# Two more parts of a modulation vector summed by VectorE instead of TensorE, in a hybrid attention, HGRN2 and MLP step

## The chip, the core and the metric

The kernel runs on one core of a Trainium2 chip. The metric is the time of one execution in microseconds (us), measured on the device; the number quoted is the median of several runs. Everything below that speaks of durations, waits or the clock comes from one profiled execution of the kernel before the change, read through views of its trace.

The engines are named as the views name them: PE is TensorE's matmuls, PEld its loads of the stationary operand, DVE is VectorE, ACT is ScalarE, POOL is GpSimd, and SP is the engine whose queue issues most transfers.

## The reference

The step takes 128 prompt tokens and 256 latent tokens (384 in all, 2048 features) through two layers. What matters here is the modulation of layer 0: six vectors of 2048 values for each of two conditioning vectors.

```python
m = jax.nn.silu(cvec) @ w_ada_l + b_ada_l              # w_ada_l: 2048 x 12288
sh1, sc1, g1, sh2, sc2, g2 = jnp.split(m, 6, axis=-1)
h = modulate(x, norm_mix, sh1, sc1)                    # rmsnorm(x) * gain * (1 + sc1) + sh1
x = x + g1 * mixer_ab(h, w_in, w_out, ...)             # attention (8 heads) beside HGRN2 (8 heads)
h = modulate(x, norm_mlp, sh2, sc2)
x = x + g2 * mlp(h, w1, w2)                            # 2048 -> 8192 -> 2048, squared ReLU
```

So SH1 and SC1 are needed first, G1 at the output projection, SH2 and SC2 at the norm ahead of layer 0's MLP, and G2 at the MLP's first outputs. Layer 1 is a pooling mixer and a second MLP. All arithmetic is in float32.

## The kernel before

The weights stream through the core once, as items of 1 MB, in a list that the host code writes out (`self.items`). Each item of a weight matrix (`w_unit`) is 1024 x 256; each of its two halves is split into a high and a low part, the high part by ScalarE (`split_hi`, L159) and the low part by VectorE (`split_lo`, L166), and TensorE then makes three products for each block of 128 features (`mm3`, L247 to L250): high by high, low by high, high by low, 384 tokens wide. Splits run four halves ahead of the products. The raw items have a ring of three buffers, the split ones five halves.

The order on every engine is the order in which the host code issues instructions; nothing reorders them. Work beside the main products sits in queues of generators (`queues`); `tick` adds a nominal time for each block of products, and a generator's next piece is issued when its yield has passed. `HY` is the yield between two steps of an HGRN2 head. A step (L859 to L868 and L841) is a chain: three products on TensorE (tile `pl`), two multiplications and one small product of totals on VectorE (`arr`, `tot`), a masked copy out of PSUM on VectorE (`att`), and a copy on ScalarE (`kh`) that the next step's products need. Attention is a longer chain for each head: scores (`s`) on TensorE, maxima on VectorE, exponentials on ScalarE, `prob` scaled on VectorE, transposes (`t`) on TensorE, copies out of PSUM by ScalarE and VectorE (`probt`), products with the values (`pov`).

The modulation's weights are items of another kind (`a_unit`) in the same list. There are two ways to sum them.

- `ada_pe`: an item is 512 rows x 512 columns; the two condition vectors are stationary and TensorE sums, in four column groups of 32 (L413, tile `psa`). One item is eight matmul records; four items make a block, 16 a part.
- `ada_dve`: an item is 256 rows x 1024 columns; VectorE multiplies and adds it into an accumulator `adaacc` of 128 x 2 x 1024, four instructions for an item (L473 for the first two of a block, L475 for the others); after eight items TensorE sums over the partitions (L489, eight records) and the result is folded (`ada_fold`).

In both, an item of this kind is handled in `split_hi`, so its instructions are issued at the start of a half of a weight item, four halves ahead of their neighbours in the list:

```python
if it["kind"] == "a":
    it["half"][half] = raw.rearrange("p (k c) -> p k c", k=k // 2)
    if "pool" not in it:
        it["proc"](half, it["half"][half])
    return
```

Before the change SH1, SC1, G1, SH2, SC2 and G2 of layer 0 all take `ada_pe`: the first two in the start-up, the other four (64 items) spread evenly between the items of the projections (`hgrn_jobs`, `att_jobs`, `gate_jobs`: 42 more items after the start-up) and of the output projection (`out_jobs`: 16 items). Layer 1's six parts take `ada_dve`, beside layer 0's MLP (`mlp_jobs`), with the accumulator in the MLP's pool.

PSUM: four accumulators `acc`, two buffers `ps_bg` shared by all background work, one `ps_s`, one `ps_a`.

Of the kernel before, what the change touches and what calls it, by code (L numbers as in the profile page):

```python
# [42 lines left out]
HY = (3.1, 3.1, 2.5, 3.1)  # L43
# [7 lines left out]
def _const_arrays():  # L51
# [28 lines left out]
    # the sums and the order of modulation rows: [block, v, group, chunk] and [block, v, chunk] -> [v, all chunks]  # L80
# [33 lines left out]
class Model:  # L114
    def __init__(self, ctx, tc, a):
        self.ctx, self.tc, self.nc, self.a = ctx, tc, tc.nc, a
        self.items = []
        self.pend = []
        self.sqs = []
        self.queues = {"e": [], "h": [], "q": [], "f": []}  # L120
        self.now = 0.0

    # ---------------------------------------------------------------- streams of weights
# [17 lines left out]
    def split_hi(self, j):  # L141
        """the high part on ScalarE; the low part's subtraction follows with split_lo."""
# [29 lines left out]
    def task(self, queue, gen, delay=0.0):  # L172
        """work beside the main products: each yield gives the time that its other engines need."""
        self.queues[queue].append([gen, self.now + delay])

    def later_on(self, fn):
        """the part of an evac that waits for ScalarE: VectorE comes to it a little later."""
# [108 lines left out]
    def quarter(self, w, c0, q, proc, pre=None):  # L286
        """half a unit: a quarter of the features, 256 columns."""
# [10 lines left out]
    def start_units(self, w, specs, pre=None):  # L298
        """the first products of a phase, a quarter of the features at a time, as these become known."""
# [50 lines left out]
    def job_tok(self, w, c0, evac):  # L350
        """out[tokens, 256 features] of w[:, c0:c0+256]."""
# [30 lines left out]
    # ---------------------------------------------------------------- adaLN  # L382
# [3 lines left out]
    def ada_done(self, layer, which, chunk0, n, ps):  # L386
        """ps [128, n, 2]: sums for n chunks of 128 features; adds the bias, folds gains in."""
# [12 lines left out]
    def ada_pe(self, layer, which, block, each=None, then=None):  # L400
        """512 columns of one part; the condition vectors are stationary, in four column groups."""
# [4 lines left out]
        def make(u):  # L406
            def proc(half, raw):
# [11 lines left out]
                if u == 3 and half == 1:  # L419
# [8 lines left out]
                    else:  # L428
                        if block == 0:
                            self.folded = self.small.tile([P, P], F32, name="folded", tag="folded", bufs=2)  # L430
                        for v in range(2):
                            at = block * 32 + v * 16
                            nc.gpsimd.dma_start(self.folded[at:at + 16], rows[v::32].rearrange("j (n c) -> j n c", n=4))
                        if block == 3:
                            self.task("f", self.ada_fold(layer, which, 0, P, self.folded), 6.5)
# [23 lines left out]
    def ada_dve(self, layer, which, block):  # L459
        """1024 columns of one part; multiply-adds on VectorE, the sum over partitions on TensorE."""  # L460
# [4 lines left out]
        def make(u):  # L465
            def proc(half, raw):
                kc = u * 2 + half
                if kc == 0:
                    st["acc"] = self.mlpp.tile([P, 2, 1024], F32, name="adaacc", tag="adaacc")
# [11 lines left out]
        def finish():  # L481
            if block == 0:
                self.folded = self.small.tile([P, P], F32, name="folded", tag="folded", bufs=2)
            folded = self.folded
            psr = self.ps_a.tile([P, 512], F32, name="psa", tag="a")
# [17 lines left out]
    # ---------------------------------------------------------------- set-up  # L503
# [922 lines left out]
```

## Time and profile before

| | |
|---|---|
| runs | 3127.81, 3128.39, 3129.56 us |
| median | 3128.39 us |
| span of the profiled execution | 3127.1 us |
| TensorE, share of the span | 98% |
| VectorE, share of the span | 58% |
| ScalarE, share of the span | 37% |
| mean granted TensorE clock | 0.996 |

The profiled span is 1.3 us under the median. Shares of busy time are averages over stages, so they tell only where to look: the projections lie at about 160 to 690 us of the span, the output projection with attention at 690 to 873 us, layer 0's MLP at 895 to 1895 us. The granted clock is a share of full speed: 1 is 2.4 GHz, 0.5 is 1.2 GHz.

### The profile page before, as it was taken

The page shows a single profiled execution, that of the slowest core. Times are in us where ns is not written, and L with a number is a line of the kernel's source. Part 1 is how long each engine was busy: PE and PEld are TensorE (multiplying, and loading weights), DVE is VectorE, ACT ScalarE, POOL GpSimd, SP SyncE. Part 2 cuts the span into 40 slices and gives each one's busy share as a digit, 9 for nine tenths or more (in the row PEclk, how much of TensorE's full clock was granted, in tenths as well). Part 3 has the DMA queues.
Part 4 walks back from the last instruction along what each step waited for, and adds up shares of the span by engine and source line. Part 5 has one row for each costly group of instructions (what it writes and reads, how often), then busy time and mean ns, then how long its engine had stood idle before and what let it go on. Part 6 is the DMA issues. An engine that isn't in the chain of part 4 may idle for free.

```text
span 3127.1 us, 43503 instructions
## 1 busy us (share of the span) xinstructions
PE 3064.3 (98%) x18106; PEld 2915.5 (93%) x18106; DVE 1821.8 (58%) x2557; ACT 1147.1 (37%) x1721; POOL 54.1 (2%) x93
## 2 busy tenths in 40 slices
PE   6999999999999999999999999899999999999997
PEld 3798889878899999999999999799999999999997
DVE  2455555545468888888978874754334343443434
ACT  3343333333362323333232333562333323233233
POOL 1100000000000000000000000000000000000000
PEclk9999999999999999999999999999999999999999
DMA  9866655565647767767767764243434434344342
GB/s 343 293 211 204 194 193 186 190 218 176 196 149 236 233 224 231 234 222 232 238 218 241 229 217 133 75 128 122 134 122 127 129 122 134 122 127 130 122 134 83
DMA packets 419460, 566.92 MB, mean 181 GB/s; under 512 B 10816, under 2 KB 338480, under 8 KB 418240
## 3 DMA queue, kind: packets, MB, share of 16 engines
q1 hardware_dynamic: 408672, 542.86, 53.6%
q0 software_dynamic: 5104, 13.65, 1.3%
q10 hardware_dynamic: 5488, 7.62, 0.8%
q8 instruction: 143, 2.34, 0.3%
q14 instruction: 53, 0.43, 0.0%
HBM read 556.13 MB, written 7.60 MB: 180 GB/s over the span
## 4 chain that ended last, share of the span: by engine, by line
PE 94%; ACT 2%; DVE 2%; DMA 1%; issue 0%; ACTq 0%; SPq 0%; DVEq 0%
PE acc L247 28%; PE acc L250 28%; PE acc L248 28%; PE psa L413 3%; PE pl L859 1%; PE acc L367 1%; PE acc L368 1%; PE acc L369 1%; ACT sp L159 1%; ACT hfull L667 0%; DVE sp L166 0%; PE acc L269 0%; PE psa L489 0%; DMA xtok<-in_x_sample 0%; PE pov L1092 0%
## 5 line engine op out<-in xcount | busy, mean ns | idle before, releaser
L159 ACT ACTIVATE sp<-raw 128x1024 fp32r<-128x1024 f32 x656 | 694.4, 1059 | 1473.9 <-PE acc L250 1204.9
L166 DVE TENSOR_TENSOR sp<-raw,sp 128x1024 fp32r<-128x1024 f32 x656 | 793.9, 1222 | 634.0 <-ACT sp L159 633.5
L247 PE MATMUL acc<-hh,sp 128*128 128x384 f32 x2720 | 923.4, 339 | 5.6 <-ACT sp L159 2.5
L248 PE MATMUL acc<-hh,sp 128*128 128x384 f32 x2720 | 910.6, 335 | 0.6 <-DVE sp L166 0.6
L250 PE MATMUL acc<-hl,sp 128*128 128x384 f32 x2720 | 691.9, 335 | 0.0
L247 PE MATMUL acc<-hid,sp 128*128 128x384 f32 x2032 | 685.7, 337 | 0.0
L248 PE MATMUL acc<-hid,sp 128*128 128x384 f32 x2032 | 683.8, 337 | 0.0
L247 PEld LDWEIGHTS acc<-hh,sp 128*128 128x128 f32 x2720 | 511.5, 188 | 51.8 <-issue 38.6
L250 PE MATMUL acc<-hid,sp 128*128 128x384 f32 x2032 | 518.6, 336 | 0.0
L248 PEld LDWEIGHTS acc<-hh,sp 128*128 128x128 f32 x2720 | 511.6, 188 | 1.0 <-DVE sp L166 1.0
L250 PEld LDWEIGHTS acc<-hl,sp 128*128 128x128 f32 x2720 | 491.8, 188 | 0.0
L475 DVE SCALAR_TENSOR_TENSOR adaacc<-raw,cpad,adaacc 128x1024 f32<-128x1024 f32 x360 | 438.4, 1277 | 0.0
L247 PEld LDWEIGHTS acc<-hid,sp 128*128 128x128 f32 x2032 | 381.4, 188 | 5.2 <-issue 5.0
L248 PEld LDWEIGHTS acc<-hid,sp 128*128 128x128 f32 x2032 | 381.4, 188 | 0.0
L250 PEld LDWEIGHTS acc<-hid,sp 128*128 128x128 f32 x2032 | 367.4, 188 | 0.0
L752 DVE SCALAR_TENSOR_TENSOR x<-acc,mods,x 128x128 f32<-128x128 f32 x576 | 200.4, 409 | 137.0 <-PE acc L250 135.1
L679 DVE TENSOR_TENSOR hid<-rsq,hid 128x384 fp32r<-128x384 f32 x128 | 65.7, 555 | 226.1 <-ACT hid L678 226.1
L413 PE MATMUL psa<-raw,cpad 128*32 128x512 f32 x768 | 112.6, 610 | 2.4 <-ACT adarow L423 1.4
L841 ACT ACTIVATE kh<-arr 128x384 f32<-128x384 f32 x56 | 31.2, 557 | 182.0 <-DVE arr L864 86.8
L864 DVE TENSOR_TENSOR arr<-arr,tot 128x384 f32<-128x384 f32 x96 | 49.2, 554 | 43.7 <-PE pl L859 42.4
L367 PE MATMUL acc<-sp,hh 128*128 128x256 f32 x240 | 73.2, 305 | 0.0
L1183 ACT ACTIVATE rsq<-relu 128x384 f32<-128x384 f32 x128 | 67.4, 526 | 4.1
(271 smaller groups left out, 2013.4 us busy)
## 6 DMA issues: line engine op xcount, KB each, us to landing
raw<-in_w_ada SPq DMA_DIRECT2D x192, 1024.0 KB, 5.1
raw<-in_w_mlp_out SPq DMA_DIRECT2D x128, 1024.0 KB, 5.4
raw<-in_w_mlp_in SPq DMA_DIRECT2D x120, 1024.0 KB, 5.6
raw<-in_w_in_ab SPq DMA_DIRECT2D x42, 1024.0 KB, 5.6
raw<-in_w_out_ab SPq DMA_DIRECT2D x16, 1024.0 KB, 5.6
raw<-in_w_in_ab POOLq DMA_DIRECT2D x17, 512.0 KB, 5.9
raw<-in_w_mlp_in SPq DMA_DIRECT2D x16, 512.0 KB, 3.7
raw<-in_w_pool SPq DMA_DIRECT2D x4, 1024.0 KB, 5.3
```

The source lines that it names most:

```text
L159: self.nc.scalar.activation(sp[:, 0], raw, AF.Copy)
L166: self.nc.vector.tensor_tensor(sp[:, 1], raw, sp[:, 0].bitcast(F32), op=ALU.subtract)
L247: mm(ps[:, :T], sp[:, 0, kc, c], hi, start=first, stop=False)
L248: mm(ps[:, :T], sp[:, 1, kc, c], hi, start=False, stop=False)
L250: mm(ps[:, :T], sp[:, 0, kc, c], lo, start=False, stop=last)
L367: nc.tensor.matmul(ps, hi, sp[:, 0, kc], start=(gk == 0), stop=False)
L413: nc.tensor.matmul(st["ps"][32 * j:32 * j + 32], self.cpad[:, kc], raw[:, k], start=(u == 0), stop=(u == 3))
L475: nc.vector.scalar_tensor_tensor(st["acc"][:, v], raw[:, 0], s, st["acc"][:, v], op0=ALU.mult, op1=ALU.add)
L679: nc.vector.tensor_tensor(lo, full, hi.bitcast(F32), op=ALU.subtract)
L752: nc.vector.scalar_tensor_tensor(self.x[:, kc, t0:t0 + n], ps[:, t0:t0 + n], g[:, kc, v:v + 1], self.x[:, kc, t0:t0 + n], op0=ALU.mult, op ...
L864: nc.vector.tensor_tensor(x, x, m, op=ALU.mult)
L1183: nc.scalar.activation(q[o], r[o], AF.Square)
```

## The change

SH2 and SC2 of layer 0 go from `ada_pe` to `ada_dve`: 32 items of 512 x 512 for TensorE become 32 items of 256 x 1024 for VectorE, in four blocks. 20 of them are spread over the 42 items of the projections, 12 over the output projection. The accumulator gets a pool of its own (`accp`), opened with the projections. G1 is spread over the projections alone; half of G2 goes to the output projection and half to the first eight items of the MLP, all by `ada_pe`. Layer 1's items end eight items before the end of the MLP instead of twelve. `HY` grows by 0.4. The sum over partitions uses a buffer of `ps_bg` instead of `ps_a`. The scratch for transfers issued by GpSimd is set to 8192 bytes. Line numbers grow by one or two.

```diff
-HY = (3.1, 3.1, 2.5, 3.1)
+HY = (3.5, 3.5, 2.9, 3.5)
...
     def ada_dve(self, layer, which, block):
...
                 if kc == 0:
-                    st["acc"] = self.mlpp.tile([P, 2, 1024], F32, name="adaacc", tag="adaacc")
+                    st["acc"] = self.accp.tile([P, 2, 1024], F32, name="adaacc", tag="adaacc")
...
         def finish():
             if block == 0:
-                self.folded = self.small.tile([P, P], F32, name="folded", tag="folded", bufs=2)
-            folded = self.folded
-            psr = self.ps_a.tile([P, 512], F32, name="psa", tag="a")
+                self.folded[layer, which] = self.small.tile([P, P], F32, name="folded", tag="folded", bufs=3)
+            folded = self.folded[layer, which]
+            psr = self.ps_bg.tile([P, 512], F32, name="psa", tag="bg")
...
     def open_mix(self):
...
+        self.accp = self.ctx.enter_context(self.tc.tile_pool(name="accp", bufs=1))
...
     def build(self):
...
-        for which in (G1, SH2, SC2, G2):
-            for b in range(4):
-                self.ada_pe(0, which, b)
...
+        def spread(body, *extras):
+            out, done = [], [0] * len(extras)
+            for n, it in enumerate(body):
+                for e, (u, lo, hi) in enumerate(extras):
+                    want = min(max(n - lo, 0) * len(u) // (hi - lo), len(u))
+                    out += u[done[e]:want]
+                    done[e] = want
+                out.append(it)
+            return out + [it for d, (u, _, _) in zip(done, extras) for it in u[d:]]
...
+        g2, norm2 = pe(G2), dve((0, SH2), (0, SC2))
+        w_in, w_out = n1 - n0, n2 - n0
+        self.items = mix[:n0] + spread(mix[n0:], (pe(G1), 0, w_in - 4), (g2[:8], w_in - 4, w_out),
+                                       (norm2[:20], 0, w_in), (norm2[20:], w_in, w_out - 2))
+        late = dve(*[(1, which) for which in range(6)])
+        self.items += spread(rest, (g2[8:], 0, 8), (late, 9, n3 - 8))
...
-    nc = _bacc.Bacc("TRN2", target_bir_lowering=False, num_devices=1)
+    nc = _bacc.Bacc("TRN2", target_bir_lowering=False, num_devices=1, dynamic_dma_scratch_size=8192)
```

The first place is VectorE's queue in the projections, in the first HGRN2 head of the second pair, where the third pair of weight columns (`hq`) is evacuated. Before:

```order
L864 TENSOR_TENSOR arr<-arr,tot 128x192x2 x2
L868 TENSOR_TENSOR tot<-tot 128x192
L846 COPY_PREDICATED att<-masks_134,pl 128x384
L166 TENSOR_TENSOR sp<-raw,sp 128x1024
L785 TENSOR_TENSOR hq<-acc,sig 128x384 x2
L864 TENSOR_TENSOR arr<-arr,tot 128x96x4 x2
L868 TENSOR_TENSOR tot<-tot 128x96
L846 COPY_PREDICATED att<-masks_134,pl 128x384
```

And of the change, in the same place:

```order
L866 TENSOR_TENSOR arr<-arr,tot 128x192x2 x2
L870 TENSOR_TENSOR tot<-tot 128x192
L848 COPY_PREDICATED att<-masks_134,pl 128x384
L477 SCALAR_TENSOR_TENSOR adaacc<-raw,cpad,adaacc 128x1024 x4
L167 TENSOR_TENSOR sp<-raw,sp 128x1024
L787 TENSOR_TENSOR hq<-acc,sig 128x384 x2
L866 TENSOR_TENSOR arr<-arr,tot 128x96x4 x2
L870 TENSOR_TENSOR tot<-tot 128x96
L848 COPY_PREDICATED att<-masks_134,pl 128x384
```

An item's four multiply-adds now stand between two steps of the head, ahead of the low part of a split, of the evacuation and of the next step.

The second place is VectorE's queue in the output projection, at the sixth attention head: the end of its softmax, the residual add of a finished pair of outputs (`x`), and the copy of transposed probabilities (`probt`). Before:

```order
L1069 TENSOR_SCALAR prob<-prob,sm 128x128
L1069 TENSOR_SCALAR prob<-prob,sm 128x384 x2
L752 SCALAR_TENSOR_TENSOR x<-acc,mods,x 128x128
L752 SCALAR_TENSOR_TENSOR x<-acc,mods,x 128x256
L752 SCALAR_TENSOR_TENSOR x<-acc,mods,x 128x128
L752 SCALAR_TENSOR_TENSOR x<-acc,mods,x 128x256
L166 TENSOR_TENSOR sp<-raw,sp 128x1024
L1083 COPY probt<-t_6231 128x384
```

And of the change:

```order
L1071 TENSOR_SCALAR prob<-prob,sm 128x128
L1071 TENSOR_SCALAR prob<-prob,sm 128x384 x2
L477 SCALAR_TENSOR_TENSOR adaacc<-raw,cpad,adaacc 128x1024 x4
L754 SCALAR_TENSOR_TENSOR x<-acc,mods,x 128x128
L754 SCALAR_TENSOR_TENSOR x<-acc,mods,x 128x256
L754 SCALAR_TENSOR_TENSOR x<-acc,mods,x 128x128
L754 SCALAR_TENSOR_TENSOR x<-acc,mods,x 128x256
L167 TENSOR_TENSOR sp<-raw,sp 128x1024
L1085 COPY probt<-t_6161 128x384
```

The four multiply-adds stand between the scaled probabilities and the copy that the products with the values wait for.

## Rows read from the trace of the kernel before

**Rows 1.** The page: busy time, share of the span, instructions.

```profile
PE 3064.3 (98%) x18106; PEld 2915.5 (93%) x18106; DVE 1821.8 (58%) x2557; ACT 1147.1 (37%) x1721; POOL 54.1 (2%) x93
```

**Rows 2.** Stages: start:end length, busy us of PE, PEld, DVE, ACT, POOL, clock, DMA.

```profile
160.00:690.00 530.00, 519.52 (x3464) 463.51 (x3463) 283.44 (x502) 188.32 (x310) 20.02 (x37) 1.00 0.61 199
690.00:873.00 183.00, 181.64 (x1050) 161.59 (x1051) 97.91 (x196) 68.58 (x123) 4.46 (x8) 0.98 0.57 182
895.00:1895.00 1000.00, 1000.00 (x5757) 985.19 (x5756) 833.95 (x928) 347.20 (x453) 9.32 (x12) 1.00 0.70 227
```

**Rows 3.** PE's waits, 160 to 690 us: in total, times, longest (first row).

```profile
PE psa L413 <- ACT adarow L423: 1.4, 2, 0.7
```

**Rows 4.** PE's waits, 690 to 873 us, and the window of its first 10 us.

```profile
PE acc L247 <- ACT mixA L678: 6.0, 1, 6.0
690.00:700.00 10.00, 8.64 (x36) 8.64 (x37) 6.67 (x16) 7.02 (x16) 0.00 (x0) 0.67 0.90 262
```

**Rows 5.** PE in order of time, projections: start, length, instruction; three HGRN2 steps.

```profile
399.61 0.83 PE L859 MATMUL pl<-arr,kh 128*128 128x128 f32 x6
...
404.47 0.83 PE L859 MATMUL pl<-arr,kh 128*128 128x128 f32 x6
405.23 1.07 PE L413 MATMUL psa<-raw,cpad 128*32 128x512 f32 x8
406.23 0.44 PE L247 MATMUL acc<-hh,sp 128*128 128x384 f32 x1
...
410.52 0.83 PE L859 MATMUL pl<-arr,kh 128*128 128x128 f32 x6
```

**Rows 6.** PE in order of time, layer 0's MLP: a sum over partitions.

```profile
995.09 1.07 PE L489 MATMUL psa<-adaacc,ones 128*32 128x512 f32 x8
996.08 0.45 PE L247 MATMUL acc<-hid,sp 128*128 128x384 f32 x1
```

**Rows 7.** DVE in layer 0's MLP: one item in order of time; L473 grouped by form.

```profile
1006.04 4.87 DVE L475 SCALAR_TENSOR_TENSOR adaacc<-raw,cpad,adaacc 128x1024 f32<-128x1024 f32 x4
...
L473 DVE TENSOR_SCALAR adaacc<-raw,cpad 128x1024 f32<-128x1024 f32 x24 | 16.9, 746 | 0.0
```

**Rows 8.** DVE, PEld and ACT in order of time: the first place shown above.

```profile
270.18 1.03 DVE L864 TENSOR_TENSOR arr<-arr,tot 128x384 f32<-128x384 f32 x2 [0.96 <-PE pl L859]
271.40 0.58 DVE L846 COPY_PREDICATED att<-masks,pl 128x384 f32<-128x384 uint8 x1
272.83 1.23 DVE L166 TENSOR_TENSOR sp<-raw,sp 128x1024 fp32r<-128x1024 f32 x1 [0.85 <-ACT sp L159]
273.98 1.01 DVE L785 TENSOR_TENSOR hq<-acc,sig 128x384 f32<-128x384 f32 x2
275.18 0.81 PEld L859 LDWEIGHTS pl<-arr,kh 128*128 128x128 f32 x6
276.21 1.02 DVE L864 TENSOR_TENSOR arr<-arr,tot 128x384 f32<-128x384 f32 x2 [1.22 <-PE pl L859]
277.35 0.53 ACT L841 ACTIVATE kh<-arr 128x384 f32<-128x384 f32 x1 [3.79 <-DVE arr L864]
280.04 0.81 PEld L859 LDWEIGHTS pl<-arr,kh 128*128 128x128 f32 x6
```

**Rows 9.** DVE, 100 to 650 us, grouped by form: one reciprocal.

```profile
L983 DVE RECIPROCAL qrow<-qrow 2x384 f32<-2x384 f32 x1 | 2.5, 2525 | 0.0
```

**Rows 10.** PE and DVE in order of time: the second place, sixth attention head.

```profile
760.35 1.06 PE L413 MATMUL psa<-raw,cpad 128*32 128x512 f32 x8
...
763.30 1.39 DVE L752 SCALAR_TENSOR_TENSOR x<-acc,mods,x 128x128 f32<-128x128 f32 x4
764.61 1.21 DVE L166 TENSOR_TENSOR sp<-raw,sp 128x1024 fp32r<-128x1024 f32 x1
766.61 0.56 DVE L1083 COPY probt<-t 128x384 f32<-128x384 f32 x1 [0.80 <-PE t L1080]
...
768.53 0.38 PE L1090 MATMUL pov<-probt,V 128*128 128x128 f32 x2
```

More of the change, by code (lines that the diff above doesn't have):

```diff
@@ L120, in __init__ @@
         self.queues = {"e": [], "h": [], "q": [], "f": []}
+        self.folded = {}
         self.now = 0.0
@@ L429, in proc @@
                         if block == 0:
-                            self.folded = self.small.tile([P, P], F32, name="folded", tag="folded", bufs=2)
+                            self.folded[layer, which] = self.small.tile([P, P], F32, name="folded", tag="folded", bufs=3)
+                        folded = self.folded[layer, which]
                         for v in range(2):
                             at = block * 32 + v * 16
-                            nc.gpsimd.dma_start(self.folded[at:at + 16], rows[v::32].rearrange("j (n c) -> j n c", n=4))
+                            nc.gpsimd.dma_start(folded[at:at + 16], rows[v::32].rearrange("j (n c) -> j n c", n=4))
                         if block == 3:
-                            self.task("f", self.ada_fold(layer, which, 0, P, self.folded), 6.5)
+                            self.task("f", self.ada_fold(layer, which, 0, P, folded), 6.5)
             return proc
@@ L482, in finish @@
             if block == 0:
-                self.folded = self.small.tile([P, P], F32, name="folded", tag="folded", bufs=2)
-            folded = self.folded
-            psr = self.ps_a.tile([P, 512], F32, name="psa", tag="a")
+                self.folded[layer, which] = self.small.tile([P, P], F32, name="folded", tag="folded", bufs=3)
+            folded = self.folded[layer, which]
+            psr = self.ps_bg.tile([P, 512], F32, name="psa", tag="bg")
             for v in range(2):
@@ L1348, in build @@
         n2 = len(self.items)
-        items, self.items = self.items, []
-        for which in (G1, SH2, SC2, G2):
-            for b in range(4):
-                self.ada_pe(0, which, b)
-        extra, self.items = self.items, []
-        merged = items[:n0]
-        body = items[n0:n2]
-        e = 0
-        for n, it in enumerate(body):
-            merged.append(it)
-            want = min((n + 1) * len(extra) // (len(body) - 2), len(extra))
-            while e < want:
-                merged.append(extra[e])
-                e += 1
@@ L1364, in build @@
-        self.items = merged
-        self.n_start = n0
-        ada1 = []
-        def collect(which, b):
-            return lambda: self.ada_dve(1, which, b)
-        for which in range(6):
-            for b in range(2):
-                ada1.append(collect(which, b))
-        m0 = len(self.items)
-        self.mlp_jobs(0, to_mlp0)
-        body, self.items = self.items[m0:], self.items[:m0]
-        keep, self.items = self.items, []
-        for go in ada1:
-            go()
-        extra, self.items = self.items, keep
@@ L1380, in build, with units, dve @@
-        e = 0
-        for n, it in enumerate(body):
-            self.items.append(it)
-            want = min(max(n - 8, 0) * len(extra) // (len(body) - 20), len(extra))
-            while e < want:
-                self.items.append(extra[e])
-                e += 1
+        def units(go, *args):
+            keep, self.items = self.items, []
+            go(*args)
+            made, self.items = self.items, keep
+            return made
+        def dve(*parts):
+            return [u for layer, which in parts for b in range(2) for u in units(self.ada_dve, layer, which, b)]
@@ new lines, in spread, with pe @@
+        def spread(body, *extras):
[7 more added lines that the diff above has]
+            return out + [it for d, (u, _, _) in zip(done, extras) for it in u[d:]]
+        def pe(which):
+            return [u for b in range(4) for u in units(self.ada_pe, 0, which, b)]
@@ L1387, in build @@
+        mix, self.items = self.items, []
+        self.mlp_jobs(0, to_mlp0)
+        n3 = len(self.items)
         self.pool_jobs()
         self.mlp_jobs(1, to_mlp1)
+        rest = self.items
+        g2, norm2 = pe(G2), dve((0, SH2), (0, SC2))
[3 more added lines that the diff above has]
+        late = dve(*[(1, which) for which in range(6)])
@@ L1389, in build @@
+        self.items += spread(rest, (g2[8:], 0, 8), (late, 9, n3 - 8))
+        self.n_start = n0
         self.run()
```

## The prediction

> **What bounds the kernel.** I read the shares first. TensorE is busy for 98% of the span, VectorE for 58% [rows 1]: the reader is to see that time on TensorE is time of the kernel and that VectorE seems to have room. The stages say the same of the places the change touches: in the projections TensorE is busy 519.5 of 530 us and VectorE 283.4, in the output projection 181.6 of 183 and 97.9 [rows 2]. Then who TensorE waits for. In the projections its waits are seven short groups, the longest 1.4 us in total [rows 3]; in the output projection there is one wait, 6.0 us for the first split of the mix [rows 4]. So work taken off TensorE's queue is gained in full, and each new wait of TensorE is lost in full, since nothing idle is left to absorb it. That makes the question one of order on VectorE: does what TensorE waits for come late there?
>
> **What is removed.** 32 items of L413 leave TensorE. Two HGRN2 steps with no item between them start 404.47 - 399.61 = 4.86 us apart; with one item, 410.52 - 404.47 = 6.05 [rows 5]. An item costs 1.19 us. The item's own records fill only 1.00 us, from 405.23 to 406.23 [rows 5]; the rest is paid at its edges. The Trainium skill (TensorEngine Tiling, Tiling Modes, Key Properties) says that changing the tiling mode drains TensorE, as these column groups of 32 do: the trace agrees with a price over the busy time. By the 1.00 us alone the saving below would be 28.0 us, by the widening 33.3. I take the widening, since it is what the next step sees. Four sums over partitions (L489) come in; their records fill the same 0.99 us [rows 6], so I charge 1.19 each. Net: (32 - 4) x 1.19 = 33.3 us off TensorE. ScalarE loses eight short copies out of PSUM and gains four; it is busy 188 of 530 us [rows 2], so nothing.
>
> **What is added on VectorE.** An item takes 4.87 us, back to back; the first of a block 2 x 0.75 + 2 x 1.22 = 3.9 [rows 7]. 20 items add 94 us to the projections (VectorE 283 to 378 of 530 us, 71%), 12 add 57 to the output projection (98 to 155 of 183, 85%). In layer 0's MLP VectorE does 834 of 1000 us with the same items and TensorE is never idle [rows 2], so the share alone does no harm. But the MLP has no chain that comes back to TensorE within a few microseconds. The projections and attention have.
>
> Take the first place shown. Before, the masked copy ends at 271.40 + 0.58 = 271.98; the split's low part follows at 272.83, the evacuation at 273.98; the next step's multiplications start at 276.21, `kh` ends at 277.88, and the following step loads it at 280.04: 2.16 us to spare [rows 8]. After, the L413 item is gone, so these multiplications would be due at 276.21 - 1.19 = 275.02. But the queue now reads: masked copy to 271.98, multiply-adds to 276.85, low part (272.83 to 273.98, 1.15) to 278.00, evacuation (1.01) to 279.01. They are 4.0 us late, 2.16 are to spare: TensorE waits 1.8 us. Behind TensorE's wait everything waits; the splits, which run four halves ahead, do not come late by a few microseconds.
>
> I did this for all 20 items, with the place of each from the order and the durations of rows 5, 7 and 8. Three have no chain behind them: 0. Two (one of them a block's first) start early enough: 0.1 each. Three stand ahead of a head's set-up: 0.7, 0.4 and 1.0. One is between two plain steps, without evacuations: 0.9. Five are like the example: 1.8, 1.8, 0.8, 2.6 and 3.9 (the last two in the third pair, whose steps lie one block of products closer). Two stand ahead of a head's last products, with the same spare time assumed: 1.9 and 0.8. Two are followed by rotary products, which need the `ps_bg` buffer that the late masked copy frees: 2.0 and 1.9. One has the key's reciprocal of 2.5 us [rows 9] in the queue as well: 2.4. One stands at the start of the last pair's token job, whose third accumulator is the one that the late evacuation of `hq` frees: 5.0. Sum 28.1 us.
>
> The output projection has six items within attention. At the second place the scaled probabilities end at 763.30; then the residual add (1.31 to the next start), the low part (1.21) and the copy of 0.56 us, which today starts at 766.61, as the transposes end, and has 768.53 - 767.17 = 1.36 us to spare [rows 10]. After: 763.30 + 4.87 + 1.31 + 1.21 (the copy waits its turn until 770.69) + 0.56 = 771.25, while the values' products are due at 768.53 - 1.19 = 767.34, the item at 760.35 being gone: 3.9 us. The other five by the same count: 2.6, 2.0, 1.4, 3.2, 3.0. Sum 16.1. The remaining six lie ahead of attention or behind it, where only residual adds follow, with a whole job of two accumulators to spare: 0, and some 3 us if that is not enough.
>
> **The clock.** The wait of 6.0 us at 690 us leaves a mean granted clock of 0.67 in the 10 us around it [rows 4], a part of it at 1.2 GHz: 10 x 0.33 = 3.3 us lost. Of the new waits only the one of 5.0 us is nearer to that than to the harmless ones under 2 us: 3.3 us more. Bounds: nothing, or 3.3 for each of the five waits of 3 us and over.
>
> **Costed at nothing.** `HY`: `mm3` advances the clock of the queues by 0.98 for a block of products, so 3.1 and 3.5 both mean four blocks, 2.5 and 2.9 three; only token jobs shift, by a third of a block. Layer 1's items ending four items later: VectorE has 166 of 1000 us free there [rows 2]. `ps_bg` for the sums: two of them fall into the projections, up to 2 us each if they wait for a buffer. G2 in the MLP's first items costs TensorE what it cost before. The smaller scratch touches GpSimd's transfers alone, and GpSimd works 20 of the 530 us [rows 2]; no row shows the scratch full, so I take nothing and, if it holds TensorE up once, at most a wait like the longest, 6 us [rows 4].
>
> **Sum.** 3127.1 - 33.3 + 28.1 + 16.1 + 3.3 = 3141.3 us of span; the median lies 1.3 above the profiled span: 3142.6 us.
>
> **The rivals.** *Cover holds (faster).* Multiply-adds wait only for their transfer. If they reach VectorE earlier than my count has it, in the idle time ahead of the half instead of behind the last step, each stalled place loses part of its delay. For: VectorE is idle nearly half of the projections [rows 2]. Against: the order puts them behind the masked copy. It decides when 32 items cost under 33.3 / 32 = 1.04 us on average; I count 44.2 / 32 = 1.4. With half the waits and no clock loss: 3128.4 - 33.3 + 22 = 3117 us; with none 3095. The Trainium skill (Perfetto Trace Analysis, Identifying the Most-Contended Engine) says to optimise the engine of highest occupancy first; by that rule alone, moving work from 98% to 58%, the 3095 would stand. Chance 0.24, between 3095 and 3122.
>
> *The two cancel (the change does nothing).* Waits of 27 to 40 us: 3122 to 3134. For: several of my items hang on one or two tenths of the 2.16 us. Chance 0.20.
>
> *The clock falls at every long wait.* Five waits of 3 us and over, 3.3 us each, 16.5 instead of 3.3, and waits a quarter above the count: 3142.6 + 13 + 11 = 3167. For: in these stages the trace has no wait between 1.4 and 6.0 us that would show where the clock starts to fall [rows 3, 4]. Chance 0.12, from 3153 up.
>
> My forecast, 3135 to 3153, has 0.44. A measurement of this kernel can tell about 0.2%, 6.3 us, from no change: faster 0.24, same 0.20, slower 0.56. The range reaches from 3108 to 3164; it leaves out the faster case's far half and the clock's far end.
>
> **What would show it.** L413 falls from 768 records to 512, L489 rises from 96 to 128. Right: PE's waits in the projections grow from a few microseconds to near 30, with `kh`, `arr`, `att` and `hq` as releasers, and near 16 in attention, released by `probt` or `prob`; the split's waits stay as they are. Wrong: those waits absent and the projections 20 us shorter; or waits for `sp` or for a transfer of `raw`, which I count at nothing. A step's spare time above 2.16 us, or an item under 4.87, would move the sum by the number of stalled places, some twenty, for each microsecond.

## The result, and the profile after

The changed kernel takes 3166.97 us (median of four runs, 3161.15 to 3168.03) against 3128.73 us for the kernel before; the ratio is 1.0119 with a 95% interval of 1.0107 to 1.0131. It is slower, as forecast, but by 38 us where 14 were forecast, and 3 us above the range. The profiled execution spans 3166.0 us, 38.9 more than the one before.

The page's first group answers to [rows 1]:

```profile
PE 3060.9 (97%) x17882; PEld 2927.2 (92%) x17882; DVE 1963.7 (62%) x2685; ACT 1145.3 (36%) x1717; POOL 49.2 (2%) x81
```

TensorE has 224 records fewer (28 items of eight), but is busy only 3.4 us less. The groups of the two kinds of item, over the whole span, before and after:

```profile
L413 PE MATMUL psa<-raw,cpad 128*32 128x512 f32 x768 | 112.6, 610 | 2.4 <-ACT adarow L423 1.4 <-DMA raw<-in_w_ada 0.9
L489 PE MATMUL psa<-adaacc,ones 128*32 128x512 f32 x96 | 12.8, 605 | 0.0
```

```profile
L414 PE MATMUL psa<-raw,cpad 128*32 128x512 f32 x512 | 79.9, 622 | 5.2 <-DMA raw<-in_w_ada 5.2
L491 PE MATMUL psa<-adaacc,ones 128*32 128x512 f32 x128 | 18.1, 605 | 3.3 <-ACT prob L1068 1.8 <-ACT sout L902 1.2
```

So the 38.9 us have three parts. The items: 79.9 - 112.6 + 18.1 - 12.8 = -27.4. All other products: -3.4 + 27.4 = +24.0, though their number is the same. TensorE's idle time: (3166.0 - 3060.9) - (3127.1 - 3064.3) = 105.1 - 62.8 = +42.3. The stages (columns as in [rows 2]):

```profile
160.00:690.00 530.00, 499.61 (x3232) 468.08 (x3230) 372.67 (x580) 185.19 (x305) 13.44 (x23) 0.98 0.54 176
690.00:873.00 183.00, 162.97 (x873) 145.36 (x874) 138.96 (x228) 62.09 (x113) 2.31 (x4) 0.94 0.58 187
```

VectorE is as busy as predicted (372.67 of 530 us, 378 worked out), and the clock column is what the prediction did not have: 0.98 and 0.94, where [rows 2] show 1.00 and 0.98.

TensorE's waits from 160 to 690 us, which answer to [rows 3] (in total, times, longest):

```profile
PE pl L861 <- ACT kh L843: 6.9, 5, 3.1
PE acc L248 <- ACT hi L794: 6.6, 4, 2.7
PE acc L368 <- DVE hq L787: 4.0, 1, 4.0
PE pqs L956 <- ACT qsq L949: 2.1, 2, 1.5
PE pqs L982 <- ACT qsq L979: 2.1, 1, 2.1
PE po L892 <- DVE arr L884: 2.0, 3, 1.4
PE pck L1028 <- DVE K L1029: 1.8, 1, 1.8
```

And from 690 to 895 us, which answer to [rows 4]:

```profile
PE pov L1092 <- DVE probt L1085: 12.0, 4, 3.6
PE acc L248 <- ACT mixA L680: 6.0, 1, 6.0
PE psa L491 <- ACT prob L1068: 1.8, 1, 1.8
PE t L1080 <- DVE prob L1071: 1.0, 1, 1.0
```

All eleven groups of the projections sum to 29.4 us. The seven of [rows 3] sum to 5.8, so 23.6 are new where 28.1 were counted. Those of attention without `mixA` sum to 14.8 (16.1 counted). The releasers named in the prediction are there, `kh`, `arr`, `hq`, `probt`, `prob`; but `hi` and `qsq`, written by ScalarE, are not on its list.

The two places that the prediction worked through. In the projections, in order of time (VectorE, then ScalarE, then TensorE):

```profile
268.83 4.86 DVE L477 SCALAR_TENSOR_TENSOR adaacc<-raw,cpad,adaacc 128x1024 f32<-128x1024 f32 x4
...
275.67 1.01 DVE L866 TENSOR_TENSOR arr<-arr,tot 128x384 f32<-128x384 f32 x2
...
276.80 0.52 ACT L843 ACTIVATE kh<-arr 128x384 f32<-128x384 f32 x1 [6.29 <-DVE arr L866]
...
277.38 0.94 PE L861 MATMUL pl<-arr,kh 128*128 128x128 f32 x6 [1.22 <-ACT kh L843]
```

The queue runs without a gap from the multiply-adds to the step's multiplications, and TensorE waits 1.22 us for `kh`: 1.8 was predicted. In attention, at the sixth head:

```profile
777.77 4.87 DVE L477 SCALAR_TENSOR_TENSOR adaacc<-raw,cpad,adaacc 128x1024 f32<-128x1024 f32 x4
...
784.99 0.55 DVE L1085 COPY probt<-t 128x384 f32<-128x384 f32 x1
...
785.68 0.46 PE L1092 MATMUL pov<-probt,V 128*128 128x128 f32 x2 [3.64 <-DVE probt L1085]
```

3.64 us, where 3.9 was predicted.

The clock around the wait for `hq` (a window of 10 us, then TensorE's rows):

```profile
520.00:530.00 10.00, 9.38 (x56) 9.39 (x57) 4.25 (x9) 1.65 (x3) 0.00 (x0) 0.67 0.24 82
```

```profile
520.62 0.58 PE L368 MATMUL acc<-sp,hh 128*128 128x256 f32 x1 [3.95 <-DVE hq L787]
521.00 0.41 PE L369 MATMUL acc<-sp,hh 128*128 128x256 f32 x1
...
526.71 0.28 PE L369 MATMUL acc<-sp,hh 128*128 128x256 f32 x1
```

The products behind the wait start 0.21 us apart and are shown with 0.41 us each; the granted clock from 522 to 524 us is 0.50, 1.2 GHz. From 526.7 they are at 0.28 again, 0.12 apart. Shorter waits do the same for a shorter time: one of 2.09 us at 293 us, of 3.06 at 472, of 2.73 at 549, and two of 0.69 and 1.45 us, at 414.6 and 576.5, that stand ahead of twelve products of two columns. Each of these costs 1.7 us: a window of 10 us shows 0.83 (at 470 below), or two neighbours share the loss, as behind the wait at 414.6:

```profile
410.00:420.00 10.00, 9.29 (x66) 8.82 (x65) 8.98 (x16) 4.73 (x8) 0.00 (x0) 0.87 0.45 144
420.00:430.00 10.00, 10.00 (x80) 8.97 (x80) 5.39 (x11) 2.71 (x3) 0.00 (x0) 0.96 0.69 231
```

The length of a wait alone does not decide it. In the same execution no fall follows waits of 1.76 us at 324, of 1.82 at 602 and of 2.15 at 927. And in e4 below, which leaves the projections as they are, the wait of 3.06 us for `kh` stands there again, but the clock stays at 1.00 (the changed kernel, then e4):

```profile
471.92 1.57 PE L861 MATMUL pl<-arr,kh 128*128 128x128 f32 x6 [3.06 <-ACT kh L843]
470.00:480.00 10.00, 8.08 (x42) 6.99 (x43) 6.28 (x13) 3.05 (x4) 0.00 (x0) 0.83 0.72 234
```

```profile
473.10 0.94 PE L861 MATMUL pl<-arr,kh 128*128 128x128 f32 x6 [3.06 <-ACT kh L843]
470.00:480.00 10.00, 6.94 (x46) 5.81 (x46) 7.90 (x15) 2.94 (x4) 0.00 (x0) 1.00 0.67 224
```

In that execution the clock falls behind a wait of 1.73 us at 324 instead. What else decides is not shown.

Over all windows of 10 us the missing share of the clock sums to 10.2 us before and 33.1 after: 23 us, about the 24.0 by which the other products grew. From 160 to 950 us it is 5.1 and 23.8: the 18.7 more are ten new falls, nine of 1.7 us and the one of 3.3 behind `hq`. The other 4.2 lie in the start-up and behind 950 us, where none of these waits stands.

### The profile page after: what moved, and what is told of

The parts are those of the page before. It is cut to its first block, busy times and chain, and to the rows that moved or that the text cites. A ratio compares the mean times of both kernels' runs of the same rounds, so it can differ in the third digit from the quotient of the medians.

```text
span 3166.0 us, 43140 instructions
## 1 busy us (share of the span) xinstructions
PE 3060.9 (97%) x17882; PEld 2927.2 (92%) x17882; DVE 1963.7 (62%) x2685; ACT 1145.3 (36%) x1717; POOL 49.2 (2%) x81
## 4 chain that ended last, share of the span: by engine, by line
PE 74%; DVE 5%; DMA 2%; ACT 2%; issue 1%; ACTq 0%; DVEq 0%; POOL 0%; POOLq 0%
PE acc L248 23%; PE acc L251 23%; PE acc L249 23%; DVE adaacc L477 1%; DVE sp L167 1%; DMA raw<-in_w_ada 1%; DVE x L754 1%; DMA raw<-in_w_in_ab 1%; ACT sp L160 0%; PE psa L491 0%; ACT hfull L669 0%; PE psa L414 0%; PE acc L270 0%; PE pov L1094 0%; DMA x<-x_spill 0%
## 5 line engine op out<-in xcount | busy, mean ns | idle before, releaser
L477 DVE SCALAR_TENSOR_TENSOR adaacc<-raw,cpad,adaacc 128x1024 f32<-128x1024 f32 x480 | 584.5, 1278 | 1.6 <-DMA raw<-in_w_ada 1.6
L248 PEld LDWEIGHTS acc<-hh,sp 128*128 128x128 f32 x2720 | 512.6, 188 | 49.6 <-issue 29.4
L414 PE MATMUL psa<-raw,cpad 128*32 128x512 f32 x512 | 79.9, 622 | 5.2 <-DMA raw<-in_w_ada 5.2
L368 PE MATMUL acc<-sp,hh 128*128 128x256 f32 x240 | 75.1, 313 | 4.0 <-DVE hq L787 4.0
L370 PE MATMUL acc<-sp,hl 128*128 128x256 f32 x240 | 69.9, 291 | 0.0
L369 PE MATMUL acc<-sp,hh 128*128 128x256 f32 x240 | 69.8, 291 | 0.0
```

Source lines behind the costliest of these rows:

```text
L248: mm(ps[:, :T], sp[:, 0, kc, c], hi, start=first, stop=False)
L368: nc.tensor.matmul(ps, hi, sp[:, 0, kc], start=(gk == 0), stop=False)
L369: nc.tensor.matmul(ps, hi, sp[:, 1, kc], start=False, stop=False)
L370: nc.tensor.matmul(ps, lo, sp[:, 0, kc], start=False, stop=(gk == KC - 1))
L414: nc.tensor.matmul(st["ps"][32 * j:32 * j + 32], self.cpad[:, kc], raw[:, k], start=(u == 0), stop=(u == 3))
L477: nc.vector.scalar_tensor_tensor(st["acc"][:, v], raw[:, 0], s, st["acc"][:, v], op0=ALU.mult, op1=ALU.add)
```

## The experiments

My theory after the result: VectorE's multiply-adds stand ahead of short chains, the stalls are the idle time, and each stall of some 2 us costs the clock besides. The rivals: the new order itself (`HY`, the list, the buffers of the sums, the scratch) holds TensorE up; or VectorE has too much work there, however it is cut. Ratios are to the kernel before, with 95% intervals.

**e1_adds_short.** In layer 0 the multiply-adds take 8 columns:

```diff
-  scalar_tensor_tensor(st["acc"][:, v], raw[:, 0], s, st["acc"][:, v], ...)
+  scalar_tensor_tensor(st["acc"][:, v, :8], raw[:, 0, :8], s, st["acc"][:, v, :8], ...)
```

> The changed kernel, but the multiply-adds of SH2 and SC2 take 8 of the 1024 columns (the first product of a block stays whole), so their sums are left out and VectorE's part of the change is nearly gone; order, transfers, sums over partitions and all else stay. If the queue on VectorE is the cause: the new waits of TensorE in the projections (some 29 us) and in attention (15) and the clock's new falls (22 us) are gone, and only the waits for G2's transfers in the MLP (4) stay: 3167 - 29 - 15 - 22 = 3101 us. If the new order of the steps (HY), the buffers of the sums over partitions or the smaller scratch hold TensorE up: not below 3128 us, and waits for kh, hq and probt are still in the list.

3129.78 us, ratio 1.0003 (0.9994 to 1.0013). The time is the rival's, the waits are not: the stalls that I laid on VectorE are gone (`kh` 0.3, `hq` 0.8, `probt` 0.8 us), and 37 us with them. But 29 us are still missing to the 3101 expected. The profiled execution is the fastest of ten, 3.3 us under the median. TensorE's longest waits in it, 160 to 670 us; behind them stand 8.9 us for `mixA`:

```profile
PE acc L248 <- ACT hi L795: 6.5, 4, 2.7
PE pqs L983 <- ACT qsq L980: 2.1, 1, 2.1
PE pbh L920 <- DVE O L916: 1.9, 2, 1.7
PE pqs L957 <- ACT qsq L950: 1.8, 3, 0.9
PE acc L248 <- ACT V L1024: 1.6, 1, 1.6
```

**e2_old_hy.** `HY = (3.1, 3.1, 2.5, 3.1)` in the changed kernel.

> The changed kernel with HY as before (3.1, 3.1, 2.5, 3.1). As I costed it, both values mean the same number of blocks for a step: 3167 us within 6. If the shift of the token jobs against the steps is what puts chains behind the multiply-adds: 10 us or more to either side, with other waits at the top of the list.

3168.51 us: `HY` costs nothing, as the prediction had it.

**e3_pairs.** The four multiply-adds issued one by one, 1.9 apart, from a queue of their own:

```diff
+  for v in range(2):
+      ...  # one multiply-add
+      yield 1.9
```

> The changed kernel, but the four multiply-adds of an item are issued one by one from a queue beside the products, 1.9 apart (two blocks of products), so that at most two of them, 2.4 us and not 4.87, stand between two steps of a chain. Work in sum is the same. If the length of what stands ahead of the chain is the cause: with 2.16 us to spare, and 1.36 in attention, waits fall from 44 to under 15 us and with no wait of 2 us the clock's new falls are gone: 3167 - 30 - 18 = 3119 us, 3105 to 3130. If VectorE's share of busy time is the cause (there is too much work beside the chains, however it is cut): 3150 us or more.

3212.2 us, ratio 1.0266 (1.0248 to 1.0283), 45 us slower than the changed kernel instead of 48 faster. Cutting the block shortens the longest wait for `kh` (1.9 us, not 3.1), but there are ten of them, 10.7 us in all, instead of five with 6.9. And ScalarE now waits 90 us for transfers in the output projection (29 in the changed kernel). The raw item is held until its last multiply-add has run. That opened the question of the buffers.

**e4_filled_waits.** Dummy products in five waits:

```diff
+        for _ in range({0: 10, 4: 8, 5: 12, 7: 8}.get(h, 0)):
+            nc.tensor.matmul(po[:, :P], self.ident, self.ident, start=True, stop=True)
...
+        self.keep_busy(20)
         self.task("q", self.attend())
```

> The changed kernel with dummy products of 128 x 128 x 128 put into five of TensorE's waits: 8 to 12 ahead of the products with the values in the four heads that waited 2.5 to 3.6 us, and 20 ahead of the first products with mixA (6.0 us). They write where the next product starts anew, so nothing computed changes. If the stand-still of TensorE is what lowers the clock: the five falls are gone, worth 1.7 us each in attention and 3.3 at mixA, 10 us in all: 3157 us, with a granted clock of 1.00 from 690 to 873 us. If the falls come from something else: 3167 us, or a little more for dummies that do not fit, with the same clock.

3161.47 us, 5.5 less. From 760 to 790 us, the changed kernel and then this one:

```profile
760.00:790.00 30.00, 23.73 (x116) 21.00 (x115) 21.16 (x36) 8.36 (x15) 1.18 (x2) 0.89 0.49 159
```

```profile
760.00:790.00 30.00, 28.26 (x177) 25.98 (x170) 22.34 (x41) 10.29 (x21) 1.18 (x2) 1.00 0.48 152
```

The waits still end when `probt` is there, but the clock stays at 1.00 behind all four. In the profiled executions of the changed kernel, e2, e6 and e19, where these waits stand whole, all four falls are there. So the stand-still is what lowers the clock in attention; that is shown. The missing clock from 700 to 950 us falls from 8.9 to 3.4 us: the four falls (6.8) and one of 1.7 at 901 are gone, a new one of 1.7 follows a wait of 1.84 us at 750, and that of `mixA` comes later. At `mixA` the dummies gained nothing; the wait that they leave is 3.7 us, and the missing clock from 690 to 710 us is 3.4 in both. That makes up 3.3 of the miss of 4 us.

**e5_short_apart, e6_apart.** No two items of the modulation are neighbours in the projections' part of the list, in e1 and in the changed kernel:

```diff
-  spread(mix[n0:], (pe(G1), 0, w_in - 4), ..., (norm2[:20], 0, w_in), ...)
+  due = [(n * 38 / 16, u) for n, u in enumerate(pe(G1))] + [(n * 42 / 20, u) for n, u in enumerate(norm2[:20])]
+  spread(mix[n0:], ([u for _, u in sorted(due, ...)], 0, w_in), ...)
```

> The run with multiply-adds of 8 columns (3130 us), with the items of G1 and of the two parts in the projections put one behind each item of weights, so that no two of them are neighbours in the list. In that run ScalarE stood 5.1, 4.8, 3.0 and 6.4 us ahead of a split whose transfer was late, each time just before it had to copy a finished accumulator, and TensorE then waited 1.66, 2.66, 0.94 and 1.59 us for hi, qsq and V. If neighbours in the list make those transfers late (two items give their buffers back together): these four waits are gone, 6.9 us, 3123 us. If TensorE waits there because the item of L413 that stood at this place is gone: the four waits stay, 3130 us.

> The changed kernel with the same new order of items in the projections, multiply-adds whole. If late transfers cost it what they cost the run of 8 columns: the waits for hi, qsq and V behind them, some 8 us, and two or three falls of the clock at 1.7 us are gone: 3155 us. The multiply-adds also stand at other places of the chains, which by my count of the places may move it by 5 us to either side. If transfers are not it: 3167 us within 5.

e5 takes 3112.94 us, ratio 0.9947 (0.9931 to 0.9964): 17 us less than e1, more than the 7 expected. ScalarE's wait for transfers of the projections' weights from 160 to 660 us, in e1 and in e5:

```profile
ACT sp L160 <- DMA raw<-in_w_in_ab: 35.2, 10, 6.5
```

```profile
ACT sp L160 <- DMA raw<-in_w_in_ab: 0.5, 1, 0.5
```

and the waits for `hi` are gone altogether. Such late transfers are not new. The kernel before, in the same stretch:

```profile
ACT sp L159 <- DMA raw<-in_w_in_ab: 25.0, 8, 6.4
```

TensorE waits only 1.9 us for `hi` and `V` there, and with a fourth raw buffer, which ends these waits of ScalarE (e18), the kernel before is 2.4 us faster, which its interval does not tell from nothing. Why a late transfer reaches TensorE in the new list and hardly in the old one is not shown.

How a late transfer reached TensorE stands in the changed kernel at 547 us, on ScalarE and then on TensorE:

```profile
547.74 1.06 ACT L160 ACTIVATE sp<-raw 128x1024 fp32r<-128x1024 f32 x1 [4.91 <-DMA raw<-in_w_in_ab]
...
548.71 0.92 ACT L794 ACTIVATE hi<-acc 128x256 f32<-128x256 f32 x3
```

```profile
549.12 0.44 PE L248 MATMUL acc<-hh,sp 128*128 128x384 f32 x1 [2.73 <-ACT hi L794]
```

The split waits for its data at the head of ScalarE's queue, the copy that frees an accumulator stands behind it, and TensorE needs the accumulator. The Trainium skill (Perfetto Trace Analysis, Tensor Engine Instruction) says that ScalarE and VectorE take their instructions strictly in order, unlike TensorE, which may pull a weight load ahead; the two ScalarE rows agree. (The description's "nothing reorders them" thus leaves out TensorE's weight loads.)

e6 takes 3165.27 us, not the 3155 that late transfers would have given: with whole multiply-adds the new order gains nothing that can be told. Its late transfers in the projections are gone too (4.5 us of waits on ScalarE), but the items stand at other places of the chains, and TensorE waits for `kh`, `arr`, `att` and `K`, up to 4.0 us at a time.

**e7_short_in_attention.** Eight columns for the twelve items of the output projection alone.

> The changed kernel, but only the twelve items in the output projection take 8 of 1024 columns (their part of SC2's sum is left out); the twenty in the projections stay whole. If each item costs where it stands: the waits for probt and prob (15 us) and the four falls of the clock there (7 us) are gone and the projections stay as they were: 3145 us. If stalls of the projections are made up for by, or passed on to, the output projection: outside 3140 to 3150 us.

3146.30 us, as expected. With e5, e1, e7 and the changed kernel there is a ladder: 3112.9, 3129.8, 3146.3, 3167.0. The order that makes transfers late, 16.9 us; the multiply-adds in the projections 16.5, those in attention 20.7. The steps hold in this sequence and do not add up in another: with whole multiply-adds the first is worth 1.7 us (e6).

**e8_sh2_free_places.** The order of the kernel before, SH2 alone on VectorE, its items at the start and the end of the projections and behind attention.

> The list of the kernel before, with the sixteen items of SH2 alone moved to VectorE and to places with little behind them: five at the start of the projections (three of these between steps of a head), four at their end, seven behind attention. G1, SC2 and G2 stay with TensorE in the projections and the output projection, 64 items in 56 places as before. If it is the place of the multiply-adds and the order of the list that cost: 14 x 1.19 = 16.7 us saved, three stalls of 1.5 us and a fall of the clock of 1.7 paid: 3118 us, 3110 to 3126. If items taken off TensorE only uncover waits that they had filled: 3128 us or more.

3142.72 us, ratio 1.0045 (1.0030 to 1.0060). That is 25 us above the forecast: my free places were not free, for the wait for `mixA` grew to 11.6 us (VectorE makes its low part), a sum waited 6.9 us for its accumulator, `x` 2.4, `kh` and `O` 2.1 to 2.9.

**e10_apart_pairs, e11_sh2_pairs, e13_pairs_ring4.** Items apart; the first half of an item is summed where it stood, the second half with the next half of a weight item (2.4 us in one piece). e11: SH2 alone, SC2 with TensorE. e13: e10 with

```diff
-SPLIT_RING = 5; AHEAD = 4; RAW_RING = 3
+SPLIT_RING = 4; AHEAD = 3; RAW_RING = 4
```

> The changed kernel with items apart (3165 us) and the four multiply-adds of an item cut in two and two: the first two where they stood, the other two one half of an item of weights later (4 us), so that the buffer of the item is given back only that much later. All sums are whole. If what stands in one piece ahead of the chain is the cause: the example of the first place is 1.6 us late instead of 4.0 with 2.16 to spare, so nearly all waits of the projections that VectorE causes are gone; in attention, with 1.36 to spare, some five waits of 1.5 us or less stay, too short for the clock: the 3113 us of the same order with 8 columns, and 6 more, 3119 us; the change would then be faster than the kernel before. If it is the sum of VectorE's work beside the chains: 3150 us or more. If buffers given back later make transfers late (as in the run with pieces 1.9 apart): splits wait longer on ScalarE than in the run of 8 columns, and 3130 to 3150 us.

> Half of the change: SH2 alone on VectorE, its sixteen items in the projections, two and two as in the run before; SC2 stays with TensorE (half of it in the projections, half in the output projection), and no item of VectorE stands in the output projection. In the projections no two items are neighbours. If the cut and the distance do there what I take them to do: 3113 us for all 32 items without VectorE's work, 14 x 1.05 back for SC2, and some 4 for the waits left: 3132 us, no better than the kernel before. If buffers given back later cost in the projections as well: 3140 us or more.

> The run with items apart and multiply-adds two and two (3181 us), with four raw buffers instead of three, paid for by four split buffers instead of five and splits three halves ahead instead of four. If raw buffers given back late make its transfers late: the waits of ScalarE for transfers (91 us in the output projection, 30 in the projections) fall to half or less, and the time by 10 us or more, to 3170 or below, in spite of the shorter lead of the splits. If the number of raw buffers is not it: those waits stay, and with the shorter lead the time is the same or longer.

3180.83, 3149.84 and 3143.29 us. e10 lies above all that I had expected, 16 us above e6, the same list with whole multiply-adds. e11 is its second branch: buffers given back later cost in the projections as well (33.1 us of ScalarE's waits for transfers there). ScalarE's waits for transfers, 160 to 880 us, in e10 and in e13:

```profile
ACT sp L168 <- DMA raw<-in_w_out_ab: 90.6, 12, 12.6
ACT sp L168 <- DMA raw<-in_w_in_ab: 29.8, 14, 4.3
```

```profile
ACT sp L168 <- DMA raw<-in_w_out_ab: 12.7, 3, 5.0
...
ACT sp L168 <- DMA raw<-in_w_in_ab: 4.1, 1, 4.1
```

With a fourth raw buffer, and in spite of the shorter lead, 104 of 120 us of these waits and 37 us of the time are gone. So in e10 the cut failed mostly by the buffers that it holds longer; for e3 this is inferred, not tested.

**e14_ring4_before, e15_ring4_after, e16_ring4_off_attention.** The same three settings in the kernel before and in the changed kernel; and e13 with four more items in the projections, eight at the end of attention and behind it, and G2's eight ahead of them.

> Control: the kernel before with four raw buffers and four split buffers, splits three halves ahead. If the fourth raw buffer only helps where VectorE gives the buffers back late: the kernel before, whose items TensorE reads, stays at 3129 us within 6. If it is a better setting for any kernel: 3120 us or less.

> The changed kernel with four raw and four split buffers, splits three halves ahead, nothing else. If neighbours in the list cost it what they did because three buffers do not hold two items and the weights behind them: the waits of ScalarE for transfers in the projections (33 us) fall to half or less, and with them the waits for hi, qsq and V (8 us) and two or three falls of the clock: 3155 us. The stalls by multiply-adds in one piece (kh, hq, probt; 24 us) stay. If VectorE's block ahead of the chains is all that matters: 3167 us.

> The best of the parts: items apart, two and two, four raw buffers (3143 us), and the twelve items of the output projection moved: four more into the projections, eight behind and at the end of attention, G2's eight ahead of them. In the run before, seven waits for probt and prob from 699 to 783 us sum to 12 us, and the clock fell there. If these come from the items that stand in attention: at most 4 us are left, 3132 us, about the kernel before. If attention waits for what the shorter lead of the splits does: 3143 us.

3143.41 us (1.0049, 1.0034 to 1.0064), 3156.70 and 3130.13 us (1.0007, 0.9997 to 1.0016). The setting costs the kernel before 15 us, and still the changed kernel gains 10. The setting changes three things at once; e18 and e19 below take the fourth buffer by itself. With most of the items off attention (e16) the change costs nothing that can be told.

**e17_ring4_full_lead, e18_before_raw4, e19_after_raw4.** `RAW_RING = 4` with the split buffers and the lead as they were; the room comes from a scratch of 2048 bytes. On e16, on the kernel before, on the changed kernel.

> The last run (3130 us) with the five split buffers and the lead of four halves given back; the room for the fourth raw buffer comes from the scratch of GpSimd's transfers (2048 bytes instead of 8192). Four split buffers and the shorter lead cost the kernel before 15 us. If they cost this one as much: 3116 us, faster than the kernel before by 0.4%, 3110 to 3122. If the smaller scratch holds GpSimd's transfers up, or the fourth raw buffer was worth less than it seemed: 3130 us or more.

> Control: the kernel before with a fourth raw buffer and scratch of 2048 bytes, five split buffers and the lead of four halves kept. If the fourth raw buffer gains only where VectorE gives buffers back late: 3128 us within 6. If it gains for TensorE's items too (three transfers in the projections came 5 to 6 us late, with waits of some 4 us behind them): 3124 us or less.

> The changed kernel with a fourth raw buffer, scratch of 2048 bytes, and nothing else. If the buffers' late return is the part of its loss that the order of the list brings: 3157 us with four split buffers, less what these cost: 3142 to 3152 us, the stalls of kh, hq and probt left. If not: 3160 us or more.

3128.82 us (1.0002, 0.9993 to 1.0011), 3126.19 us (0.9993, 0.9984 to 1.0002) and 3155.05 us (1.0086, 1.0070 to 1.0101). The kernel before does not care, for the buffer or for the scratch, which speaks against the scratch as a cause; the changed kernel regains 12 of its 38 us by a buffer alone, 3 us short of the range expected. e17 missed: the lead given back was worth nothing that can be told, and no version here that makes all the sums beats the kernel before.

## Why the prediction was wrong

**The step that failed: the clock.** "Of the new waits only the one of 5.0 us is nearer to that than to the harmless ones under 2 us: 3.3 us more." Measured: 18.7 us from 160 to 950 us, in ten falls, and 22.9 over the span. In these stages the trace of before had single waits of 0.9 us and less (the 1.4 us of [rows 3] are two of 0.7) and the one of 6.0, and I drew a line between them by distance. There is no such line in the runs: falls followed waits of 1.59 us (e1 at 582), 1.73 and 1.84 (e4), and none followed waits of 2.15 us (the changed kernel at 927), 2.66 (e1 at 532) and 3.06 (e4 at 473). With 18.7 in place of 3.3 the sum of the prediction gives 3158, with 22.9 it gives 3162. In terms of the span the miss is 24.7 us: 20.7 by which the other products grew beyond the clock's 3.3, 5.9 by the removal, less 1.9 by the waits. The rival *The clock falls at every long wait*, to which I gave 0.12, priced 3167. It had the mechanism, but not its size: it had five falls of 3.3 us, and there are ten, nine of them of 1.7; its other 11 us were for more waiting, which did not come. That its time came out is luck.

**The removal: -33.3 predicted, -27.4 measured.** The price of 1.19 us was read between two steps of a head. Over the whole span an item's records are worth 1.02 us (32.7 / 32), nearer to the 1.00 that I turned down. A saving at the edges would show in the neighbouring products; those grew by 24.0 us where the missing clock grew by 22.9, so none is to be seen. And "work taken off TensorE's queue is gained in full" did not hold everywhere: in the kernel before an item stood between the last product of a token job and the next job's accumulator, and TensorE waited 0.51 us for `hi` behind it; in the changed kernel nothing stands there at 199 us and TensorE waits 1.07. Even e5, with VectorE's work left out and transfers on time, saves only 16 us.

**The waits: 44.2 predicted, 42.3 of idle time measured, but in part for other reasons.** The two places that I worked through came within 0.6 us. The waits for the releasers that I had named, and for `K`, sum to 29.5 us in the changed kernel and to 2.7 in e1: by this count VectorE's stalls are 26.8 us, not 44.2. The idle time as a whole falls by only 20.9 us in e1 (105.1 - 84.2, its span of 3124.7 less 3040.5 busy), mainly since `mixA` waits 2.9 us longer there. Between e1 and e5 it falls by another 12.9 (84.2 - 71.3, its span of 3111.2 less 3039.9): transfers made late by neighbours in the list. The last 8.5 (71.3 - 62.8) are above all G2's transfers, `mixA`, `hq` and `qsq`; that items had covered such waits before is read from the rows, not shown. I had costed all this at nothing, and had named "waits for `sp` or for a transfer of `raw`" among what would prove me wrong; they came through ScalarE, as waits for `hi`, `qsq` and `V`. So the sum agreed by chance: the stalls by VectorE were counted too high, another term was left out. The list holds 40 items of weights behind the start-up's part of the projections, not 42 as the description says; the counts per item do not hang on it.

**G2 in the MLP's first items**, costed at what it cost before, brought three waits of 4.2 us in all for its transfers. The sums over partitions, costed at up to 2 us each, waited 1.2 us in the projections and 1.8 in attention.

**Right:** VectorE's share, the direction, the order on VectorE as the reason, the releasers `kh`, `hq`, `probt`, `prob`, and `HY` at nothing (e2). The Trainium skill (Perfetto Trace Analysis, Identifying the Most-Contended Engine) says to optimise the most contended engine first, and for TensorE it goes by the work done and the busy share of weight loads, not by that of the products. Here the share of weight loads (93%) points to TensorE as that of the products does (98% [rows 1]), but the section does not say that work moved off it is gained in full: the 3095 was the prediction's own reading, and 3167 was measured.

**Open.** Why e17 gains nothing from the lead that costs the kernel before 15 us. Why `mixA` waits 6.0 us in the changed kernel and 8.7 to 8.9 in e1 and e7, which have the same list. The best version still has 20 us of missing clock against 10 before. That the fall needs the waits is shown in attention (e4); for the projections it is read from the rows alone, and which of the waits lower the clock differs from run to run. G2's new place was not tested by itself.

## What to carry to other kernels

Before moving work to an engine that is half idle, look at its longest uninterrupted piece beside the shortest spare time of any chain that runs through its queue, and at what the moved work holds while it waits: here three raw buffers, which were in nobody's sum. Price a stall of the tensor engine with the clock behind it: here 18.7 us on some 38 us of new waits, about half as much again. And test a saving by leaving the added work out: that run (e1) showed nothing to win in the list as it stood, and 16 us with the items apart (e5), not 33.

## What the runs showed that I had not expected

- Ten waits, seven of 2.1 to 3.6 us, one of 3.95 and two of 0.69 and 1.45 us ahead of twelve products of two columns, were followed by products at 1.2 GHz; each cost 1.7 us, the longest 3.3. The same wait of 3.06 us lowered the clock in one execution and not in another. Eight to twelve dummy products in four waits of attention kept the clock at 1.00.
- In the list of e1, with neighbouring items of 1 MB in a ring of three buffers, ScalarE's splits waited for transfers ten times, up to 6.5 us, 35 us in 500; with the items set apart, 0.5 us.
- Cutting a block of 4.87 us into pieces made the changed kernel 14 to 45 us slower. For the cut in two (e10) a fourth buffer took 37 us off, so there it was the buffer given back later.
